# A denominator moved ahead of the turn of the carries in slots 12 and 13 of an RWKV kernel

## The chip, the cores and the metric

The kernel runs on one core of a Trainium2 chip. The metric is the device time of one execution in microseconds (us). Before the change it is 290.88 us, the median of three runs (291.6, 290.88, 290.25). The profile is that of one execution whose span is 289.9 us; all times inside the profile are counted from the start of that span.

The engines are named as in the profile: PE is the matmul engine and PEld its weight loads, DVE is VectorE, ACT is ScalarE, POOL is GpSimd and SP is SyncE. L553 stands for line 553 of the kernel.

## The reference

The inputs are `k` and `v` of shape (16, 2048, 256) and per-channel vectors `w` and `u`. For each batch and channel a recurrence runs over the 2048 steps, with a numerator `aa`, a denominator `bb` and a running maximum `pp` in the exponent:

```python
for t in range(seq_len):
    ww = u + kk
    qq = np.maximum(pp, ww)
    e1 = np.exp(pp - qq); e2 = np.exp(ww - qq)
    output[b, t, :] = (e1 * aa + e2 * vv) / (e1 * bb + e2 + 1e-08)
    ww = pp - w + kk
    qq = np.maximum(ww, kk)
    e1 = np.exp(ww - qq); e2 = np.exp(kk - qq)
    aa = e1 * aa + e2 * vv
    bb = e1 * bb + e2
    pp = qq
```

## The kernel before

The sequence is cut into a head of 32 steps and 16 stretches ("steps" of the kernel, numbered c) of 126 time steps. A stretch is worked on in four tiles of four batches each. With the two tiles of the head there are 66 tiles, numbered n: 0 and 1 are the first two of stretch 0, 2 and 3 the head, 4 and 5 the rest of stretch 0, 6 to 9 stretch 1, 10 to 13 stretch 2, and so on. The main loop runs through *slots*; slot n starts the work on tile n and finishes that on tiles some nine slots older.

What is done for one tile:

- `round_k` (DVE, L315) rounds k; `logs` (PE, L331, tile X) forms the exponents by two matmuls for each half; `exps` (ACT, L347) takes their exponentials into the tile `ez`; `times_v` (DVE, L354) multiplies by v.
- `sums` (PE, L385) adds the tile up for the carries of its stretch.
- `den` (PE, L553) forms the denominators; `log_den` (ACT, L565) and `invert` (ACT, L570) turn them into reciprocals; `num` (PE, L578 for each half) forms the numerators; `mult` (DVE, L588) multiplies, and `store` writes out.

The carries of a stretch are worked out from its sums by small operations on DVE and ACT (L422 to L495), ending in `carries` (DVE, tile `ab`, L495). They are then turned by a matmul, copied out as a `row`, and sent by small transfers into two spare rows (126 and 127) of the `ez` tiles of that stretch, so that `den` and `num` of those tiles, which read all 128 rows, take the carries in:

```python
def turn_carries(c):
    d = bank("num", [128, D]) if wide else bank("den", [128, 2, D])[:, 0]
    K(PE.matmul(d[:, 0:128], st.pop((c, "ab")).rearrange("p m q x -> p (m q x)"), It, start=True, stop=True))
    st[c, "d"] = d

def inject(c):
    row = small.tile([128, 128], BF16, tag="row", name="row")
    K(DVE.tensor_copy(row, st.pop((c, "d"))[:, 0:128]))
    for j in range(c == 0, 2):
        for h in range(2):
            p = 64 * h + 32 * j
            K(SP.dma_start(out=EZ[group_of(c, j)][TC + h:TC + h + 1, 0:2, :, :].rearrange(
                               "o q i (x c) -> o (q i x) c", c=128),
                           in_=row[p:p + 32, :]))
```

Here `EZ[group]` holds two tiles. For stretch 1 the first two transfers (j = 0) go to tiles 6 and 7, the other two to tiles 8 and 9.

Three things write to the same buffer `den` in on-chip accumulation memory: `den` itself, the turn of the carries, and a turn of the sums (L403). The pool has one buffer of it (`psd`, bufs=1) until the loads are over:

```python
def den(n):
    rl, ri = (NH, NH) if is_head(n) else (TC if is_direct(n) else 128, TC)
    d = bank("den", [128, 2, D])
    for m, r, q in (((Lh if is_head(n) else Lf), rl, 0), (Id, ri, 2)):
        for i in range(tiles_of(n)):
            K(PE.matmul(d[:, i, :], m[0:r, :], ez_of(n)[0:r, q, i, :], start=q == 0, stop=q == 2, ...))
    # ... (tiles 0 and 1 alone add their carries here, by further small matmuls)
    DEN[n] = d
```

`K` pins the order of the instructions of each engine to the order in which the program writes them. The slot loop writes them so (cut):

```python
LAG = 9
out_at = {n + (LAG - 3 if is_head(n) else LAG + 1 if n < 2 else LAG): n for n in range(NP)}
for n in range(NP + LAG + 1):
    q, qi, qp = out_at.get(n), out_at.get(n - 1), out_at.get(n - 2)
    ...
    small_work(n, "a3")
    if live:
        exps(n)
    small_work(n, "d0")
    if more and n > EARLY:
        round_k(n + 1)
    small_work(n, "p0")
    if out_qp:
        num(qp, 0)
    small_work(n, "d1"); small_work(n, "a0"); small_work(n, "p1")
    if out_qi and qi < NP - 1:
        invert(qi)
    small_work(n, "a2")
    if out_q:
        if q not in DEN:
            den(q)
        log_den(q)          # ... (cut: the last slots)
    if out_qp:
        mult(qp, 0)
    small_work(n, "d2"); ...; small_work(n, "d3"); small_work(n, "a4")
    if more:
        logs(n + 1)
    if live and out_qp:
        num(qp, 1)
    small_work(n, "p3")
    if live:
        times_v(n)
        sums(n)
    small_work(n, "p2"); small_work(n, "d4")
    if out_qp:
        mult(qp, 1)
        store(qp)
    small_work(n, "d5"); small_work(n, "p4"); small_work(n, "a1")
```

The small operations of the carries are put in by plans, as (slots after the stretch's last tile, place in the slot, function). For most stretches the plan ends so:

```python
"steady": (..., (3, "d4", carry_weights), (3, "d5", carries), (3, "p4", turn_carries), (4, "d0", inject),
           (4, "d2", state_add, 1), (4, "d4", state_decay, 1)),
```

The last tile of stretch 1 is tile 9. So its carries are made and turned at the end of slot 12, and the row is copied at the start of slot 13. By `out_at`, the denominators come in these slots: tile 0 in slot 10, tile 1 in slot 11, none in slot 12, tile 4 in slot 13, tile 5 in slot 14, tile 6 in slot 15, and from there one in each slot.

Of the kernel before, what the change touches and what calls it, by code (L numbers as in the profile page):

```python
# [22 lines left out]
def kernel(  # L23
# [593 lines left out]
    def at(slot, where, f, *args):  # L617
        later.setdefault((slot, where), []).append((f, args))
# [27 lines left out]
    for c in range(-1, NST):  # L646
        for slot, where, f, *args in PLANS["head" if c < 0 else "first" if c == 0 else
                                           "last" if c + 1 == NST else "steady"]:

            if f is copy_sums and 0 < c < NST - 1:  # L650
                where, args = "d1", (DVE,)
            at(last_of[c] + slot, where, f, c, *args)
    at(0, "d1", matrices_for_head)
    at(4, "d4", matrices_for_outputs)
    at(5, "d4", matrices_for_outputs_of_head)
    at(6, "d4", more_matrices_for_outputs)
# [121 lines left out]
```

## Time and profile before

| What | Value |
|---|---|
| Time, median of three runs | 290.88 us (290.25 to 291.6) |
| Span of the profile | 289.9 us |
| Start of the exponentials of tiles 12, 13, 14, 15, 16 on ACT | 45.74, 48.98, 53.29, 56.91, 60.99 us |
| Turn of the carries of stretch 1 on PE | 50.57 us |
| Copy of the row on DVE | 50.84 us |
| den(4), den(5), den(6): first matmul | 51.29, 54.19, 58.44 us |
| HBM traffic over the span | 352 GB/s |

A line of the timeline gives the start, the duration, the engine, the line of the kernel, the operation, the tiles (written <- read), the shapes and the count. A bracket at the end gives the time for which the engine had been idle before it and what ended that idle time. Busy time is not the same as being the bound: an engine with idle time between its instructions may still set the end by a wait, and one that is busy may lie beside the path.

### The profile page before, as it was taken

Reading aid. Unit: us, or ns where it says so; the run is one execution under the profiler, and the core shown is the slowest. Engines: PE = TensorE matmul, PEld = TensorE weight load, DVE = VectorE, ACT = ScalarE, POOL = GpSimd, SP = SyncE. Lnnn points to the kernel's source line nnn. Section 1 sums busy time; section 2 is a strip of 40 time slices with the busy share of each in tenths; the row PEclk is TensorE's granted clock in tenths of the full one; section 3 lists DMA queues with packets and bytes.
Section 4 is the critical chain, followed back from the end, with each engine's and each line's share of the span. In section 5 each row is a group of like instructions: output and inputs, shape, how many; then the busy total and the mean of one; then the engine's idle time right before and its main releaser. Section 6 shows DMA issues by size and latency. Waiting matters only on the chain.

```text
span 289.9 us, 4117 instructions
## 1 busy us (share of the span) xinstructions
PE 253.2 (87%) x1194; PEld 119.2 (41%) x1210; DVE 254.4 (88%) x529; ACT 265.5 (92%) x298; POOL 161.1 (56%) x227
## 2 busy tenths in 40 slices
PE   8888988998989998989989898989898998988950
PEld 3334444544434444434444444444343444433420
DVE  6598899899999999999999999999999999978760
ACT  7957989799999999999999999999999999998970
POOL 8695546746656666556566655666565652122530
PEclk9999999999999999999999999999999999999995
DMA  6999999999999999999999999999999999345875
GB/s 180 243 271 296 304 308 302 261 305 332 323 330 307 342 335 329 332 337 342 345 336 326 330 332 342 339 337 328 336 329 332 326 308 279 132 149 197 279 244 152
DMA packets 58971, 85.95 MB, mean 296 GB/s; under 512 B 6746, under 2 KB 43090, under 8 KB 58948
## 3 DMA queue, kind: packets, MB, share of 16 engines
q0 software_dynamic: 52672, 81.99, 102.0%
q1 hardware_dynamic: 5978, 3.41, 4.6%
q10 hardware_dynamic: 298, 0.27, 0.3%
q8 instruction: 10, 0.16, 0.2%
q14 instruction: 13, 0.11, 0.1%
HBM read 68.12 MB, written 34.05 MB: 352 GB/s over the span
## 4 chain that ended last, share of the span: by engine, by line
DVE 41%; DMA 24%; PE 15%; issue 9%; ACT 4%; POOL 3%; DVEq 0%; POOLq 0%; ACTq 0%
DMA vr<-in_v_dram 21%; DVE ez L354 17%; DVE rd L588 11%; DVE km L315 5%; PE num L578 5%; PE X L331 3%; DMA out_dram<-rd 3%; PE den L553 3%; ACT rd L565 2%; PE tot L385 2%; PE den L403 2%; DVE S L427 1%; DVE spread L540 1%; DVE ab L495 1%; DVE da L465 1%
## 5 line engine op out<-in xcount | busy, mean ns | idle before, releaser
L347 ACT ACTIVATE ez<-X 128x2048 bf16<-128x2048 f32 x58 | 108.7, 1874 | 0.4 <-PE X L331 0.4
L588 DVE TENSOR_TENSOR rd<-num,rd 128x512 f32<-128x512 f32 (+2 forms) x131 | 88.7, 684 | 4.4 <-ACT rd L570 3.6
L143 POOL DMA_DIRECT2D vr<-in_v_dram x64 | 48.9, 764 | 73.1 <-DVE ez L354 36.7
L354 DVE TENSOR_TENSOR ez<-ez,vr 126x2048 bf16<-126x2048 bf16 (+1 forms) x66 | 79.7, 1209 | 2.6 <-DMA vr<-in_v_dram 2.6
L608 POOL DMA_DIRECT2D out_dram<-rd x63 | 56.2, 892 | 39.5 <-issue 11.0
L565 ACT ACTIVATE rd<-den 128x1024 f32<-128x1024 f32 (+3 forms) x67 | 66.9, 998 | 4.6 <-PE den L553 2.6
L570 ACT ACTIVATE rd<-rd 128x1024 f32<-128x1024 f32 (+3 forms) x67 | 69.4, 1035 | 0.3
L578 PE MATMUL num<-ez,LfN 128*128 128x512 bf16 (+1 forms) x128 | 49.2, 384 | 7.6 <-DVE rd L588 7.6
L331 PE MATMUL X<-km,NLE 128*128 128x512 f32 x128 | 50.6, 477 | 2.2 <-DVE km L315 1.0
L578 PE MATMUL num<-ez,IdN 126*128 126x512 bf16 (+1 forms) x131 | 49.8, 380 | 0.0
L121 POOL DMA_DIRECT2D kr<-in_k_dram x60 | 45.7, 761 | 6.1 <-issue 2.4
L315 DVE CAST km<-kr 126x1024 fp32r<-126x1024 f32 x64 | 47.5, 742 | 0.9 <-DMA kr<-in_k_dram 0.8
L331 PE MATMUL X<-km,NLZ 128*128 128x512 f32 x128 | 40.4, 396 | 0.2 <-ACT ez L345 0.2
L553 PE MATMUL den<-ez,Id 126*128 126x512 bf16 (+1 forms) x131 | 39.1, 378 | 0.8
L553 PE MATMUL den<-ez,Lf 128*128 128x512 bf16 (+1 forms) x112 | 34.6, 378 | 0.1
L385 PE MATMUL tot<-ez,OHV 126*32 126x512 bf16 x128 | 25.2, 384 | 5.2 <-DVE ez L354 5.1
L331 PEld LDWEIGHTS X<-km,NLE 128*128 128x128 f32 x128 | 23.2, 189 | 13.7 <-ACT lf L422 1.3
L331 PEld LDWEIGHTS X<-km,NLZ 128*128 128x128 f32 x128 | 24.0, 188 | 6.2 <-ACT ez L345 0.6
L385 PE MATMUL tot<-ez,OHE 128*32 128x512 bf16 x128 | 25.2, 390 | 0.0
L578 PEld LDWEIGHTS <-LfN 128*128 128x128 bf16 (+1 forms) x128 | 12.3, 96 | 22.9 <-issue 20.5
L553 PEld LDWEIGHTS <-Lf 128*128 128x128 bf16 (+1 forms) x128 | 12.4, 98 | 18.7 <-issue 7.1
L553 PEld LDWEIGHTS <-Id 126*128 126x128 bf16 (+1 forms) x131 | 12.7, 97 | 15.7
(113 smaller groups left out, 213.2 us busy)
## 6 DMA issues: line engine op xcount, KB each, us to landing
out_dram<-rd POOLq DMA_DIRECT2D x60, 512.0 KB, 7.4
kr<-in_k_dram POOLq DMA_DIRECT2D x56, 512.0 KB, 8.0
vr<-in_v_dram POOLq DMA_DIRECT2D x60, 256.0 KB, 7.3
kr<-in_k_dram SPq DMA_DIRECT2D x4, 512.0 KB, 5.0
kr<-in_k_dram POOLq DMA_DIRECT2D x4, 504.0 KB, 9.3
out_dram<-rd POOLq DMA_DIRECT2D x3, 504.0 KB, 6.8
vr<-in_v_dram POOLq DMA_DIRECT2D x4, 252.0 KB, 8.0
ez<-row SPq DMA_DIRECT2D x62, 8.0 KB, 5.2
```

Source lines behind the costliest of these rows:

```text
L143: K(POOL.dma_start(out=vr_of[n][0:r, :, :], in_=v[4 * p:4 * p + 4, t0:t0 + r, :].rearrange("n t d -> t n d")))
L315: K(DVE.tensor_copy(KM[n][0:r, 0:i, :], kr_of.pop(n)[0:r, 0:i, :]))
L331: K(PE.matmul(X[q][:, i, :], m[0:kr, :], km[0:kr, i, :], start=True, stop=True))
L347: K(SC.activation(ez_of(n)[:, 0:4:2], X[2][:, :, 0:i, :], ACT.Exp))
L354: K(DVE.tensor_mul(ez[0:r, 1:4:2], ez[0:r, 0:4:2], vb[0:r].unsqueeze(1).broadcast_to([r, 2, i, D])))
L385: K(PE.matmul(TOT[c][y:y + 32], m[0:r, :], ez_of(n)[0:r, q, i, :], start=n == first_of[c], stop=n == last_of[c] or (head and i == 1), tile ...
L553: K(PE.matmul(d[:, i, :], m[0:r, :], ez_of(n)[0:r, q, i, :], start=q == 0, stop=q == 2, skip_group_check=True))
L565: K(SC.activation(RD[n][0:r, a:b, :], DEN[n][0:r, a:b, :], ACT.Ln, scale=RS))
L570: K(SC.activation(RD[n][0:r, a:b, :], RD[n][0:r, a:b, :], ACT.Exp, scale=-1.0))
L578: K(PE.matmul(d, m[0:r, :], ez_of(n)[0:r, q, i, :], start=q == 1, stop=q == 3, skip_group_check=True))
L588: K(DVE.tensor_mul(RD[n][0:r, i, :], NUM.pop((n, i))[0:r, :], RD[n][0:r, i, :]))
L608: K(eng.dma_start(out=out[4 * p + a:4 * p + b, t0:t0 + r, :].rearrange("n t d -> t n d"), in_=o[0:r, a:b, :]))
```

## The change

In stretch 1 alone, the turn of the carries moves from the end of slot 12 to slot 13, behind num(1,1), and the copy of the row moves with it, behind `times_v(13)`. The denominator of tile 4 moves from the middle of slot 13 to the end of slot 12, ahead of the turn. As both use the one den buffer, the turn now follows the log of that denominator, where before the denominator followed the copy of the row. It is for the wait in which ACT stands before the log of den(4). No instruction is added or removed.

```diff
         for slot, where, f, *args in PLANS["head" if c < 0 else "first" if c == 0 else
                                            "last" if c + 1 == NST else "steady"]:
 
+            if c == 1 and f in (turn_carries, inject):
+                slot, where = 4, "p3" if f is turn_carries else "d4"
+
             if f is copy_sums and 0 < c < NST - 1:
                 where, args = "d1", (DVE,)
             at(last_of[c] + slot, where, f, c, *args)
     at(0, "d1", matrices_for_head)
+    at(12, "p2", den, 4)
     at(4, "d4", matrices_for_outputs)
```

The order of the instructions on PE changes so, from the sums of tile 12 to those of tile 13:

```
before: sums(12), turn, num(1,0), den(4), logs(14), num(1,1), sums(13)
after:  sums(12), den(4), num(1,0), logs(14), num(1,1), turn, sums(13)
```

and on DVE, from the carries to the rounding of tile 15:

```
before: carries, copy of the row, round_k(14), mult(1,0), state_add, times_v(13), state_decay, mult(1,1), round_k(15)
after:  carries, round_k(14), mult(1,0), state_add, times_v(13), copy of the row, state_decay, mult(1,1), round_k(15)
```

ACT has the same order in both.

## The prediction

> **What bounds the kernel now.** I read the busy line first, then the busy time by stretch, then the order of time around slot 13, engine by engine, and last the four small transfers that carry the turned carries.
>
> ```profile
> PE 253.2 (87%) x1194; PEld 119.2 (41%) x1210; DVE 254.4 (88%) x529; ACT 265.5 (92%) x298; POOL 161.1 (56%) x227
> ```
>
> The busy time by stretch (us, then busy us of PE, PEld, DVE, ACT, POOL, clock, DMA share, GB/s):
>
> ```profile
> 40.00:45.74 5.74, 5.23 (x32) 2.54 (x31) 5.23 (x13) 4.66 (x7) 3.71 (x5) 1.00 1.24 306
> 45.74:53.29 7.55, 6.16 (x39) 3.46 (x38) 7.12 (x15) 6.00 (x8) 4.97 (x8) 1.00 1.07 259
> 53.29:60.99 7.70, 7.37 (x40) 3.35 (x39) 6.35 (x13) 7.70 (x10) 3.95 (x6) 1.00 1.14 286
> 76.80:92.60 15.80, 14.48 (x70) 6.93 (x69) 14.96 (x30) 15.69 (x20) 9.62 (x12) 1.00 1.16 318
> 92.60:108.40 15.80, 14.48 (x70) 6.94 (x69) 14.86 (x30) 15.50 (x18) 9.74 (x12) 1.00 1.17 336
> ```
>
> The reader is to see that ACT (ScalarE) is the bound from 53 us on: 7.70 of 7.70 us, then 15.50 to 15.69 of 15.80 us for each four slots, at the same pace to 250 us. So time lost or won on ACT near slot 13 should stay to the end. The one large hole of that region lies in 45.74 to 53.29, where ACT is busy 6.00 of 7.55 us. ACT in order of time:
>
> ```profile
> 48.98 1.86 ACT L347 ACTIVATE ez<-X 128x2048 bf16<-128x2048 f32 x1
> 52.36 1.03 ACT L565 ACTIVATE rd<-den 128x1024 f32<-128x1024 f32 x1 [1.52 <-PE den L553]
> 53.29 1.88 ACT L347 ACTIVATE ez<-X 128x2048 bf16<-128x2048 f32 x1
> ```
>
> These are the exponentials of tile 13, the log of denominator 4, and the exponentials of tile 14. The hole is 1.52 us, ended by den(4). What den(4) waits for is seen on DVE and PE:
>
> ```profile
> 48.36 1.22 DVE L354 TENSOR_TENSOR ez<-ez,vr 126x2048 bf16<-126x2048 bf16 x1
> 50.23 0.28 DVE L495 TENSOR_TENSOR ab<-AB,phi 128x128 bf16<-128x128 f32 x1
> 50.84 0.29 DVE L508 CAST row<-den 128x128 bf16<-128x128 f32 x1 [0.33 <-PE den L503]
> 51.64 0.68 DVE L588 TENSOR_TENSOR rd<-num,rd 128x512 f32<-128x512 f32 x1
> 52.37 1.22 DVE L354 TENSOR_TENSOR ez<-ez,vr 126x2048 bf16<-126x2048 bf16 x1
> 53.96 0.69 DVE L588 TENSOR_TENSOR rd<-num,rd 128x512 f32<-128x512 f32 x1 [0.24 <-PE num L545]
> ```
>
> ```profile
> 49.63 0.39 PE L385 MATMUL tot<-ez,OHV 126*32 126x512 bf16 x2
> 50.57 0.23 PE L503 MATMUL den<-It,ab 128*128 128x128 bf16 x1 [0.54 <-DVE ab L495]
> 51.72 0.60 PE L553 MATMUL den<-ez,Id 126*128 126x512 bf16 x2
> 52.62 0.63 PE L331 MATMUL X<-km,NLZ 128*128 128x512 f32 x2
> ```
>
> The turn of the carries (L503) uses the only den buffer, and it idles PE for 0.54 us until the carries (L495) are made. DVE copies the turned row out (L508, ends 51.13), and only then may den(4) write: it ends at 52.32 and X(14) at 53.25.
>
> **The other end of the row.** The row goes by four 8 KB transfers from SyncE into ez, the first two for tiles 6 and 7. Their first reader is den(6) in slot 15:
>
> ```profile
> 58.44 0.59 PE L553 MATMUL den<-ez,Lf 128*128 128x512 bf16 x2
> ```
>
> The queries for the row's transfers, over the whole run:
>
> ```profile
> L512 SPq DMA_DIRECT2D ez<-row x62: 502/590/1206, 34.4 to 268.5; - x62
> DMA to landing us min/median/max: 1.9/5.2/6.9
> ```
>
> Asked one by one, the four of this step are issued at 51.19, 51.74, 52.44 and 53.45 and take 4.4, 4.7, 6.9 and 6.8 us. So the pair that den(6) needs is there at 51.74 + 4.7 = 56.4, and den(6) starts at 58.44: **slack 2.0 us**. This is the number on which I decide.
>
> [...] behind the waiting turn, num(1,0) stands still although its bank came free at 50.31. So a den(6) that waits holds X(16) behind it. [...] the same 8 KB take 4.4 to 6.9 us here and as little as 1.9 us at the end, when loads are over.
>
> **The change part by part.** No instruction is added or removed. Three things move.
>
> 1. den(4) (4 matmuls) goes from slot 13 to the end of slot 12, ahead of the turn, where its buffer has been free since the log of den(1) ended at 45.52. The sums of tile 12 begin their last pair at 49.63; elsewhere the next matmul starts 0.32 us after that pair (57.04 to 57.37), so den(4) starts at 49.95. Matmuls of this width start 0.22 us apart (58.44, 58.65, 58.87, 59.09), so the last starts at 50.61 and ends at 50.99. The log can start at 51.03, not 52.36: ACT waits about 0.2 us, not 1.52.
>
> 2. PE then runs num(1,0) (two of 0.22 us and four short ones of 0.055) from 50.83; X(14) starts at about 51.5 and ends after 1.2 us (55.40 to 56.56 elsewhere), at 52.7. exp(14) starts at 52.75, not 53.29: **0.54 us won on ACT**. It is less than the hole, as X(14) becomes the limit; it is the 0.54 us for which PE stood idle.
>
> 3. DVE loses its wait of 0.33 us and the copy of 0.29, but then waits for num(1,0), which ends at 51.65, not 51.45. The product at 51.64 starts at 51.69, and the product with v (52.37) at 52.42. The copy of the row now comes after that one, at 53.55 to 53.85; the turn itself, behind num(1,1) on PE, is ready at about 53.4, and the log that it must follow ended at 52.1, so the wait in the title costs nothing. The product at 53.96 starts at 53.88: DVE wins 0.08 us. X(15) waits for k rounded on DVE, so at exp(15) only 0.1 to 0.3 of the 0.54 us is left.
>
> 4. **The price.** The row is ready at 53.85, not 51.13: 2.7 us later, against a slack of 2.0. Transfers start at 53.91 and 54.46. With 4.7 us the second lands at 59.2; with 5.8, the median of the four, at 60.3; with 6.9, like those issued in this very stretch (52.44, 53.45), at 61.4. den(6), ready at about 58.36, then starts at 59.2, 60.3 or 61.4.
>
> 5. From den(6) to ACT: it needs 1.03 us (58.44 to 59.47), the log follows 0.04 us later, and exp(16) starts 1.22 us after the log (59.77 to 60.99, with two small exponentials between). So exp(16) starts 2.29 us after den(6): at 61.5, 62.6 or 63.7, against 60.99 now. That is **0.5, 1.6 or 2.7 us lost**. The 0.54 us won lies before this wait and is swallowed by it. The second pair, for tiles 8 and 9, would land at 62 to 63 and is read in slot 17 (66.99): no wait.
>
> After slot 16 ACT is full, so what is lost there stays; perhaps 0.1 to 0.2 us comes back, as ACT has idle bits of 0.2 us at 68.05 and 74.69. I take the middle, 1.6, less 0.2, and lean toward the short landing, since the first pairs of later steps take 4.7 to 5.2 us where the trace has their landing (82.9 to 210 us): about +1.2 us. 290.88 + 1.2 = 292.1.
>
> **Rivals.** *The hole is simply filled.* exp(14) wins 0.54 us and all behind it moves up: 290.4, or 290.7 if DVE's 0.1 to 0.3 us is what survives. For it: ACT is the bound, with 7.70 of 7.70 us. Against it: the row must land within 3.9 us of its second issue, and under load none of the first pairs did (4.4 us is the shortest I looked at near this step). *Given back without a loss.* The landing takes about 4.4 us and den(6) stands only some 0.5 us; exp(16) is then within 0.2 us of now: 290.9. *A longer wait.* The transfers meet the bulk loads and take 6.9 us: 293.4. *The turn waits for the log of den(4).* It would idle PE, but the log ends 1.1 us before PE comes to the turn: no effect.
>
> **Range and chances.** From a short landing (+0.3) to a long one (+2.5) with repeats that themselves spread from 290.25 to 291.6: 290.8 to 293.4. Two per cent are 5.8 us, which none of the cases reaches: within 2% at 0.98, faster and slower 0.01 each. Within these 2%, I give four in five to a small loss.
>
> **What would show it.** The wait of 1.52 us before the log at 52.36 shrinks to about 0.2 us; exp(14) starts near 52.75; the copy of the row starts near 53.5; PE has a new idle of 0.8 to 2.9 us before den(6), ended by the row's transfer; exp(16) starts at 61.5 to 63.7; from there the pace is again 15.8 us for four slots. I am wrong if den(6) starts before 58.9, which needs the row copied before 53 us or a landing in about 4 us, or if the delay at slot 16 melts away by 100 us.

## The result and the profile after

The changed kernel takes 295.98 us (median of six runs, 294.07 to 296.61), against 290.86 us before (six runs, 290.25 to 291.6): a ratio of 1.0166 with a 95% interval of 1.0134 to 1.0199. It is slower by 5.1 us: a loss within two per cent, as foretold, but larger than the prediction allowed (292.1, at most 293.4). The ratios, here and below, are worked out from single runs, without those over 1.5% above the fastest of their kernel, and so are not quotients of the medians.

The busy line of the changed kernel's page, and its busy time by stretch (columns as before). The first two stretches run from exp(12) to exp(14) and to exp(15), the third from there to exp(16); the fourth lies in the steady part:

```profile
PE 254.6 (86%) x1194; PEld 119.9 (41%) x1210; DVE 254.5 (86%) x529; ACT 266.2 (90%) x298; POOL 160.3 (54%) x227
```

```profile
45.10:52.04 6.94, 6.10 (x38) 3.37 (x37) 6.26 (x14) 6.10 (x8) 4.08 (x7) 1.00 1.14 274
52.04:55.89 3.85, 3.58 (x21) 1.64 (x20) 3.85 (x7) 3.73 (x3) 3.11 (x5) 1.00 1.11 268
55.89:64.85 8.96, 5.30 (x19) 2.63 (x17) 3.88 (x8) 4.36 (x6) 2.36 (x4) 0.73 1.14 315
96.00:112.00 16.00, 14.67 (x70) 7.04 (x70) 15.03 (x31) 15.69 (x18) 9.82 (x13) 1.00 1.17 338
```

Nearly all the harm lies in the third line. From exp(15) to exp(16) took 4.08 us before (56.91 to 60.99) and takes 8.96 us now, with every engine but PE idle for more than half of it, and with a mean PE clock of 0.73. ACT of the changed kernel in order of time:

```profile
50.40 1.02 ACT L565 ACTIVATE rd<-den 128x1024 f32<-128x1024 f32 x1 [0.20 <-PE den L553]
52.04 1.88 ACT L347 ACTIVATE ez<-X 128x2048 bf16<-128x2048 f32 x1 [0.62 <-PE X L331]
...
63.14 1.02 ACT L565 ACTIVATE rd<-den 128x1024 f32<-128x1024 f32 x1 [4.23 <-PE den L553]
...
64.85 1.88 ACT L347 ACTIVATE ez<-X 128x2048 bf16<-128x2048 f32 x1 [0.37 <-PE X L331]
```

The hole of 1.52 us before the log of den(4) is gone (0.20 us, then 0.62 us for X(14)). In its place ACT waits 4.23 us before the log of den(6). DVE and PE show the way there:

```profile
51.05 0.69 DVE L588 TENSOR_TENSOR rd<-num,rd 128x512 f32<-128x512 f32 x1 [0.57 <-PE num L545]
51.79 1.22 DVE L354 TENSOR_TENSOR ez<-ez,vr 126x2048 bf16<-126x2048 bf16 x1
52.93 0.28 DVE L508 CAST row<-den 128x128 bf16<-128x128 f32 x1
53.26 0.69 DVE L588 TENSOR_TENSOR rd<-num,rd 128x512 f32<-128x512 f32 x1
```

```profile
57.35 0.38 PE L578 MATMUL num<-ez,IdN 126*128 126x512 bf16 x1
61.24 1.01 PE L553 MATMUL den<-ez,Lf 128*128 128x512 bf16 x2 [3.50 <-DMA ez<-row]
62.04 1.06 PE L553 MATMUL den<-ez,Id 126*128 126x512 bf16 x2
62.54 1.41 PE L331 MATMUL X<-km,NLE 128*128 128x512 f32 x2
```

The row is copied at 52.93. PE is through with num(4,0) at 57.73 and stands 3.50 us until the row has landed. Then each pair of den matmuls takes 1.01 to 1.06 us, where it took 0.59 and 0.60 before. The clock of PE (second column from the left is the length; the last three are clock, DMA share and GB/s) fell to half inside the wait, at 60.06 us:

```profile
59.00:60.00 1.00, 0.00 (x0) 0.00 (x0) 0.93 (x5) 0.00 (x0) 0.00 (x0) 1.00 1.29 281
60.00:61.00 1.00, 0.00 (x0) 0.00 (x0) 0.87 (x1) 0.00 (x0) 0.00 (x0) 0.53 1.09 392
63.00:64.00 1.00, 1.00 (x4) 0.81 (x3) 0.00 (x0) 0.86 (x1) 0.00 (x0) 0.50 1.33 306
```

That last row must be read with care: PE is "busy" for the whole microsecond, but at a clock of 0.50 the two X matmuls begun at 62.54 take 1.41 us, where the like pair at 103.45, at a clock of 1.00, takes 0.80. The transfers of the row, asked for the first pair alone:

```profile
L512 SPq DMA_DIRECT2D ez<-row x2: 503/1024/1545, 53.3 to 53.8; - x2
...
DMA to landing us min/median/max: 5.7/6.5/7.3
```

The second one is issued at 53.82 and takes 7.3 us: it lands at 61.10. In the kernel before it took 4.7 us. The bulk load issued just ahead of it (v of tile 19, issued at 53.31) lands at 61.06, within 0.04 us of it.

### The profile page after: what moved, and what is told of

It reads as the page before. It is cut to its first block, busy times and chain, and to the rows that moved or that the text cites. A ratio compares the mean times of both kernels' runs of the same rounds, so it can differ in the third digit from the quotient of the medians.

```text
span 294.9 us, 4116 instructions
## 1 busy us (share of the span) xinstructions
PE 254.6 (86%) x1194; PEld 119.9 (41%) x1210; DVE 254.5 (86%) x529; ACT 266.2 (90%) x298; POOL 160.3 (54%) x227
## 4 chain that ended last, share of the span: by engine, by line
DVE 39%; DMA 25%; PE 15%; issue 10%; ACT 7%; POOL 1%; DVEq 0%; SPq 0%; POOLq 0%; ACTq 0%
DMA vr<-in_v_dram 17%; DVE ez L354 15%; DVE rd L588 10%; DVE km L315 5%; PE num L578 5%; DMA out_dram<-rd 3%; ACT rd L565 3%; PE den L553 3%; PE X L331 3%; DMA ez<-row 2%; DMA kr<-in_k_dram 2%; ACT ez L347 2%; PE tot L385 2%; DVE ab L495 1%; PE den L403 1%
## 5 line engine op out<-in xcount | busy, mean ns | idle before, releaser
L608 POOL DMA_DIRECT2D out_dram<-rd x63 | 55.6, 882 | 46.4 <-issue 12.1
L565 ACT ACTIVATE rd<-den 128x1024 f32<-128x1024 f32 (+3 forms) x67 | 66.9, 998 | 9.1 <-PE den L553 5.3
L331 PE MATMUL X<-km,NLE 128*128 128x512 f32 x128 | 51.2, 482 | 2.7 <-ACT ez L345 0.8
```

Source lines behind the costliest of these rows:

```text
L331: K(PE.matmul(X[q][:, i, :], m[0:kr, :], km[0:kr, i, :], start=True, stop=True))
L565: K(SC.activation(RD[n][0:r, a:b, :], DEN[n][0:r, a:b, :], ACT.Ln, scale=RS))
L608: K(eng.dma_start(out=out[4 * p + a:4 * p + b, t0:t0 + r, :].rearrange("n t d -> t n d"), in_=o[0:r, a:b, :]))
```

## The experiments

Theory A is that of the prediction: the row now reaches tiles 6 and 7 too late for den(6), and what follows from that wait is the whole loss. Theory B is that the new order on PE and DVE itself costs. The kernel before was run beside each group and takes 291.35 to 291.36 us there (25 to 39 runs); ratios are against it.

**Late send.** The order of the kernel before stays; only the transfers go out late, from a holding tile.

```diff
 def inject(c):
+    if c == 1:  # copied out of the den buffer at the old time
+        st["held"] = tiny.tile([128, 128], BF16, tag="held", name="held")
+        K(DVE.tensor_copy(st["held"], st.pop((c, "d"))[:, 0:128]))
+    else:
+        send(c)
+
+def send(c):
     row = small.tile([128, 128], BF16, tag="row", name="row")
-    K(DVE.tensor_copy(row, st.pop((c, "d"))[:, 0:128]))
+    K(DVE.tensor_copy(row, st.pop("held") if c == 1 else st.pop((c, "d"))[:, 0:128]))
     # ... the transfers
+at(13, "d4", send, 1)
```

> The kernel before, with its order of den(4) and turn untouched; the turned row of stretch 1 is copied out of the den buffer at the old time, into a holding tile, and a second small copy at the place where the changed kernel copies (behind the product with v of slot 13) feeds the four transfers. Only the time of sending is late, by about 2.5 us; added is one copy of 128x128 on DVE, about 0.1 to 0.2 us. Theory A (the late landing before den(6), with the PE clock that drops behind the wait, is the cost): PE idle 2.5 to 4 us before den(6), and 294.5 to 296.5 us. Theory B (the new order on PE and DVE, with den(4) ahead and the turn behind num(1,1), is the cost): no more than 0.2 us over the kernel before, 290.9 to 291.2.

Measured: 295.58 us, ratio 1.0127 (1.0083 to 1.0170). The added copy takes 0.19 us. PE of this run before den(6):

```profile
61.78 0.68 PE L560 MATMUL den<-ez,Lf 128*128 128x512 bf16 x2 [3.69 <-DMA ez<-row]
62.25 1.06 PE L560 MATMUL den<-ez,Id 126*128 126x512 bf16 x2
```

The old order with a late row has the whole loss, the wait and the slow pair behind it. Theory B falls.

**No read.** The changed kernel, but den and num of tiles 6 and 7 read 126 rows. It leaves the carries of stretch 1 out of these two tiles, so that nothing waits for the row there.

```diff
-rl, ri = (NH, NH) if is_head(n) else (TC if is_direct(n) else 128, TC)
+rl, ri = (NH, NH) if is_head(n) else (TC if is_direct(n) or n in (6, 7) else 128, TC)
```

> The changed kernel, where den and num of tiles 6 and 7 read 126 rows in place of 128 and so leave the carries of stretch 1 out of these two tiles; their first reader then waits for no transfer. Theory A: the idle time before den(6) is gone, exp(14) stays about 0.6 us early, and the time is 290.3 to 290.8, 0 to 0.5 us under the kernel before. Theory B (the new order): still 294 to 296.

Measured: 290.95 us, ratio 0.9982 (0.9966 to 0.9997). PE at the same place:

```profile
57.39 0.38 PE L578 MATMUL num<-ez,IdN 126*128 126x512 bf16 x1
57.76 0.59 PE L553 MATMUL den<-ez,Lf 126*128 126x512 bf16 x2
```

No wait, and no loss, though the row was no quicker (it took 7.3 us and landed at 61.18). So the wait of den(6) and what hangs on it is all the harm. As control, the same edit in the kernel before:

> A control: the kernel before, where den and num of tiles 6 and 7 read 126 rows and so leave the carries of stretch 1 out of these tiles. The kernel before had no wait for the transfers, so this should change nothing: within 0.2 us of it. Then the 0.4 us that the changed kernel without this wait was under the kernel before are what the filled hole is worth; if the control is 0.4 us under it too, the filled hole is worth nothing.

Measured: 291.16 us, ratio 0.9985 (0.9953 to 1.0017). The control is as far under the kernel before as the changed kernel without its wait. So these runs show no gain in time from the filled hole.

**Turn only.** One part alone: without `at(12, "p2", den, 4)`, so that den(4) stays in slot 13.

> One part of the change alone: the turn and the copy of the row go to slot 13 as in the changed kernel, den(4) stays at its old place behind num(1,0). Theory A: the row is as late as in the changed kernel, so the time is the same within 0.5 us, 295.3 to 296.5; the log of den(4) starts some 0.7 us later than in the changed kernel but exp(14), bound by X(14), at the same time. If it is the early den(4) that costs: back at 291.

Measured: 295.54 us, ratio 1.0126 (1.0089 to 1.0163). The early den(4) is harmless; the late turn has the loss. One part of the expectation failed: exp(14) starts 7.28 us after exp(12), against 6.94 with the early den(4) and 7.55 before. So more than half of the time won at exp(14), 0.34 of 0.62 us, comes from the early den(4), and not all from the late turn.

**Clock held.** The changed kernel with matmuls of zeros in the wait: `at(15, "a2", idle, psd, 12)`.

> The changed kernel with 12 matmuls of zeros (2.6 us at 0.22 us each) put on PE right ahead of den(6), where it stands idle for 3.5 us. If the drop of the PE clock to half behind that wait is a cost of its own: den(6) again takes about 1.0 us in place of 1.9, exp(16) follows 2.3 us after den(6) in place of 3.6, and the time is 1.0 to 1.4 us under the changed kernel, 294.6 to 295.0. If the clock does not matter to the path (ACT would be late anyway): within 0.3 us of the changed kernel.

Measured: 294.95 us, ratio 1.0103 (1.0072 to 1.0134). In its profile the row came still later than in the changed kernel (8.5 us, at 62.31), and yet:

```profile
57.73 2.75 PE L219 MATMUL idle<-zeros 128*128 128x512 bf16 x12
62.45 0.38 PE L553 MATMUL den<-ez,Lf 128*128 128x512 bf16 x1 [1.97 <-DMA ez<-row]
62.88 0.59 PE L553 MATMUL den<-ez,Id 126*128 126x512 bf16 x2
```

The pair takes 0.59 us again, and exp(16) follows den(6) by 2.30 us in place of 3.61. (One record of the first pair is missing here.) So 1.3 us of the changed kernel's profile are the clock. To see it in time, both stand once more in one group:

> The changed kernel once more, as it is, beside the three others of this group. Theory A says: PE stands 2.5 to 4 us before den(6) again, ended by the second transfer at about 61 us. Open is the loss of 1.1 us between 220 and 250 us in the first profile, where ACT waits for buffers of results not yet stored: if it belongs to the change it comes again, if it is chance it does not. 294.5 to 296.5 us.

> The 12 matmuls of zeros ahead of den(6) once more, now beside the changed kernel itself: if the broken PE clock costs, 0.8 to 1.4 us under the changed kernel of this group, and 2.3 us from den(6) to exp(16) in the profile; if not, within 0.3 us.

Measured: the changed kernel 294.60 us (six runs, 292.72 to 296.29), ratio 1.0116 (1.0071 to 1.0161); with zeros 293.87 us (ten runs), ratio 1.0089 (1.0058 to 1.0119). The difference of 0.7 us has the expected sign, but the intervals overlap: in time the cost of the clock is not settled. One reason is seen in the profile of the changed kernel of this group, which is its shortest run:

```profile
60.45 0.59 PE L553 MATMUL den<-ez,Lf 128*128 128x512 bf16 x2 [1.96 <-DMA ez<-row]
60.88 0.60 PE L553 MATMUL den<-ez,Id 126*128 126x512 bf16 x2
```

Here the row took 5.7 us, PE stood 1.96 us and kept its clock. So the two profiles of the changed kernel differ in how long the transfer takes and in whether the clock breaks. The mean PE clock of whole runs suggests how often it breaks: it is 0.988 in this run and 0.974 to 0.984 in the changed kernel's eleven others, as in the profiles with a broken clock (0.978 to 0.983); in all sixteen runs with zeros it is 0.987 to 0.992.

**Why is the landing so late?** Three runs move the sending or what is issued beside it. The first is the late send with the second copy ahead of the product with v (`at(13, "d2", send, 1)`):

> The kernel before with the holding tile, where the second copy and the transfers come ahead of the product with v of slot 13, some 1.2 us later than in the kernel before and 1.2 us sooner than in the late send. If a transfer took 4.7 us as in the kernel before, the second would land near 57.6, before den(6) at 58.44: 290.9 to 291.3. If the transfers sent from 52.4 us on land at 59.3 to 60.3 whatever they are (as the third and fourth did in the kernel before, 6.9 us), den(6) stands 1 to 2 us: 292 to 293.5. So the slack was less than 2.0 us if it is the second.

Measured: 294.17 us, ratio 1.0076 (1.0042 to 1.0109). That is above what I expected. The row was sent 0.8 us sooner than in the late send, took 6.5 us and landed at 60.65; PE stood 1.74 us, and its clock broke (0.60 in the mean from 61 to 62 us, 0.50 in the two behind), which my expectation left out. After exp(12), this row lands 2.0 us sooner than that of the late send, but no sooner than that of the changed kernel's second profile (14.56 against 14.46 us), which is sent 0.7 us later. One profile of each can't tell what the sooner sending is worth.

The second is the changed kernel with the turn right behind `logs(14)` and the copy ahead of `times_v(13)`:

```diff
-slot, where = 4, "p3" if f is turn_carries else "d4"
+slot, where = 4, "p5" if f is turn_carries else "d6"   # p5: behind logs(n + 1); d6: ahead of times_v(n)
```

> The changed kernel with the turn right behind the matmuls of X(14) and the copy of the row ahead of the product with v of slot 13: the row is sent about 0.9 us sooner, DVE does its copy before the product. Theory A: the second transfer lands 0.5 to 1 us sooner than in the changed kernel (near 60.3), PE stands about 2.5 us, and the time is 293.5 to 295.

Measured: 292.48 us (the seven runs of the ratio, 290.69 to 294.43; two more took 295.12 and 295.51), ratio 1.0036 (0.9999 to 1.0073), somewhat better than I expected. The profile is that of the longest run, which the ratio leaves out; its row landed at 60.85. That the row came in time in the short runs is likely, but no profile shows it.

The third holds back the bulk loads:

```diff
+if n == 15:
+    load(19)
+    load(20)
-if n + AHEAD < NP:
+if n + AHEAD < NP and n not in (13, 14):
     load(n + AHEAD)
```

> The changed kernel, where the loads of tiles 19 and 20 are issued behind the store of tile 1 (with those of tile 21) in place of slots 13 and 14: about 0.75 MB less is queued ahead of the row's transfers. If their 5.7 to 8.5 us are the bulk loads queued with them: the second lands within 5 us of its issue, PE stands less than 1.1 us before den(6) with its clock unbroken, and the time is 290.3 to 292. If the length comes from elsewhere (the two rows, the SyncE issue): 6 us and more as before, and 295 to 296.5.

Measured: 291.68 us, ratio 1.0014 (0.9995 to 1.0033). POOL of the changed kernel, from the loads of tile 19 to the next store, and then of this run:

```profile
52.26 0.77 POOL L121 DMA_DIRECT2D kr<-in_k_dram  x1
53.31 0.75 POOL L143 DMA_DIRECT2D vr<-in_v_dram  x1 [0.27 <-DVE row L508]
54.52 0.76 POOL L608 DMA_DIRECT2D out_dram<-rd  x1 [0.47 <-issue]
```

```profile
51.95 0.76 POOL L608 DMA_DIRECT2D out_dram<-rd  x1
54.95 0.75 POOL L608 DMA_DIRECT2D out_dram<-rd  x1 [2.23 <-ACT ez L347]
```

Its first pair of transfers, and den(6):

```profile
L512 SPq DMA_DIRECT2D ez<-row x2: 502/870/1237, 53.7 to 54.3; - x2
...
DMA to landing us min/median/max: 4.4/4.6/4.7
```

```profile
58.76 0.59 PE L553 MATMUL den<-ez,Lf 128*128 128x512 bf16 x2 [0.60 <-DVE km L315]
```

Nothing was changed about the row. With no load issued between 51.95 and 54.95 it lands at 58.63, in place of 61.10. The profile names DVE for the wait of 0.60 us, but den(6) starts 0.13 us after the landing. The last bulk transfer now issued ahead of it, the store at 51.95, landed at 58.26. So with the loads of tile 19 issued just ahead of it the transfer took 7.3 us, and without them 4.4 us. Both together:

> Both of the former, the sooner turn and the held loads. If both act on the landing and add up: it lands by 57.5, no wait before den(6), and the time is 290.2 to 291.0, at or a little under the kernel before; the most that the filled hole on ACT gave without any wait was 0.4 us (290.95 against 291.36).

Measured: 291.42 us, ratio 1.0001 (0.9985 to 1.0017). The row lands at 57.67 and den(6) does not wait. The whole loss is gone, and nothing is won, where I had expected 290.2 to 291.0. The control, held loads in the kernel before:

> A control for the held loads: the kernel before with the loads of tiles 19 and 20 held back in the same way. Its row had 2.0 us to spare and the loads are needed only four to five slots later: within 0.3 us of the kernel before. If it is faster by 0.3 us or more, the held loads themselves help, and the sum of sooner turn and held loads hides a loss of the change.

Measured: 290.99 us (the 21 runs of the ratio), ratio 0.9982 (0.9961 to 1.0003): no difference that these runs can show. Here the second transfer took 6.8 us in spite of the held loads. It is sent at 51.18, before the loads of tile 19 would be issued; those of tile 18, issued 1.5 and 0.7 us ahead of it, stayed. No version beat the kernel before clearly.

The profiles side by side, in us after the start of exp(12), which takes out how the first slots of each run went (the kernel before: exp(12) at 45.74):

| Kernel | second transfer sent | landed | PE idle before den(6) | den(6) to exp(16) | exp(16) |
|---|---|---|---|---|---|
| before | 6.00 | 10.72 | 0 | 2.55 | 15.25 |
| before, no read | 6.00 | 12.94 | (not awaited) | 2.54 | 15.26 |
| before, held loads | 6.00 | 12.76 | 0.20 | 2.35 | 15.25 |
| changed | 8.72 | 16.00 | 3.50 | 3.61 | 19.75 |
| changed, again | 8.72 | 14.46 | 1.96 | 2.30 | 16.89 |
| changed, turn only | 8.91 | 15.38 | 2.70 | 3.30 | 18.81 |
| before, late send | 8.79 | 16.55 | 3.69 | 3.27 | 19.96 |
| before, mid send | 8.03 | 14.56 | 1.74 | 3.23 | 17.93 |
| changed, clock held | 8.72 | 17.21 | 1.97, behind 12 zeros | 2.30 | 19.65 |
| changed, clock held, again | 8.71 | 15.87 | 0.64, behind 12 zeros | 2.30 | 18.31 |
| changed, held loads | 8.71 | 13.09 | 0.60 | 2.30 | 15.52 |
| changed, sooner and held | 7.91 | 12.63 | 0 | 2.31 | 15.26 |
| changed, no read | 8.72 | 16.04 | (not awaited) | 2.38 | 15.01 |

den(6) is needed 12.6 to 12.7 us after exp(12). Where the clock breaks, den(6) to exp(16) is 3.2 to 3.6 us, elsewhere 2.3 to 2.55.

## Why the prediction was wrong

**The way was right.** The order of events came as foretold, and the steps on the engines to within 0.1 us. From exp(12), the log of den(4) was predicted at 5.29 us and came at 5.30; the copy of the row at 7.81, and came at 7.83; the product behind it 0.08 us sooner than before, and came 0.06 us sooner. I gave 0.54 us to exp(14), and 0.62 came. What is lost at slot 16 stays, as foretold: the exponentials of the changed kernel's profile run 4.15 to 4.17 us behind those of the kernel before from 73 to 223 us.

**The step that failed is the fourth, "The price": the landing.** I laid three cases side by side, 4.7, 5.8 and 6.9 us, took the middle one and then leaned "toward the short landing", because later steps took 4.7 to 5.2 us. In the six profiles that send at the changed kernel's time with the loads as they are (changed, clock held twice, no read, late send, and changed again) the transfer took 7.3, 8.5, 7.2, 7.3, 7.8 and 5.7 us: five of the six are above the longest case. In turn only, sent 0.2 us later, it took 6.5 us. The transfers sent nearest to that moment in the trace of the kernel before (52.44 and 53.45, 6.9 and 6.8 us) were the better model, not the pairs of later steps. With the loads of this stretch held back, the transfer took 4.4 us; why those of later steps were quicker is not shown. (By that step's own landings PE would stand 0.8 to 3.0 us before den(6), not 0.8 to 2.9.)

The middle case did come, in the second profile of the changed kernel: the row landed 14.46 us after exp(12), where the middle case has 14.6, exp(16) came at 16.89, where it has 16.9, and that run took 292.72 us. The eleven other runs of the changed kernel took 293.94 us or more. So the case that I took as the middle was near the lucky end.

**The slack was not a number but a draw.** I decided on 2.0 us, from one profile. With the same order and the same moment of sending, the no-read control landed at 12.94 us where 12.7 are needed, and the control with held loads at 12.76, so that den(6) stood 0.20 us. So the old moment of sending leaves at times no slack at all, though no profile of the kernel before itself shows that. (Two of its 39 runs in the last group took 294.2 and 294.41 us, with a mean PE clock of 0.983 and 0.984 like the changed kernel's; why is not shown.)

**The fifth step, den(6) to ACT, was mis-sized where the wait is long.** I took 2.29 us, which came where PE kept its clock (2.30). In the first profile it was 3.61 us: behind 3.50 us of standing still, PE ran at half its clock until 66.9 us. The length of standing still alone does not decide in these runs: 1.96 us kept the clock, 1.74 us broke it, and so did 2.70, 3.50 and 3.69. The slow stretch is 6.83 us long in the first profile (60.06 to 66.89), and about 3.4 us in turn only and in mid send, worked out from the mean clock of each microsecond. What sets the moment at which the clock breaks is not shown. I had the wait in view and forgot its second effect.

So the first profile's exp(16), 19.75 us after exp(12) where the middle case has 16.86, is 2.89 us too late for two reasons: den(6) starts 1.6 us later than in that case, as the landing took 7.3 us and not 5.8, and the way from den(6) to exp(16) is 1.3 us longer, by the broken clock.

**The sum of the first profile**, exp(12) to exp(16): den(6) starts 3.44 us later than before (16.14 against 12.70), and from there to exp(16) is 1.06 us longer (3.61 against 2.55): 4.50 us, which is 19.75 less 15.25. Of the rest of the 5.0 us between the two spans, 0.64 us is taken off by a quicker start before slot 12, and some 1.1 us comes after exp(16), mostly from 227 us on, where ACT waits 1.7 us in all for buffers of results not yet stored. This did not come again in the second profile of the changed kernel. It stood in the profiles with a broken clock (0.2 to 1.7 us), but also in one whose clock was whole and which has no loss, the no-read control (0.8 us). So it is not shown to belong to the change; why it comes is open.

**The rivals.** "The hole is simply filled" fell in both ways: den(6) waits, and without that wait the gain melts. In the no-read run exp(14) is 0.62 us early, exp(15) 0.38, exp(16) 0.24 and exp(20) 0.07 (31.21 us after exp(12) against 31.28), probably because DVE and PE are nearly as full as ACT (86%, 86% and 90% of the first profile's span); no run tests that. The 0.1 to 0.3 us that I left at exp(15) was near, but I had not followed it to the end. "Given back without a loss" needed a landing in about 4.4 us; that came with the held loads alone, and there den(6) stood 0.60 us and the time was not clearly longer (1.0014). "A longer wait" (6.9 us, 293.4) was the one that held, and was still too short. The turn behind the log cost nothing, as foretold.

## What to carry to other kernels

- When a change makes a producer later, look at the far end of what it feeds before the near end: a gap of 1.5 us was filled, and a transfer that seemed to have 2.0 us to spare became a wait of 2.0 to 3.5 us.
- The time of a small transfer beside bulk loads was no constant here: 5.7 to 8.5 us in six profiles. Take it from transfers issued near the same moment, from several profiles, and take the long ones for the slack.
- The new wait on PE was charged twice in the profiles where the clock broke behind it (den(6) to exp(16) took 3.2 to 3.6 us, and 2.3 where it held), and its length alone did not tell whether it would: 1.74 us broke the clock, 1.96 us did not. And a gap on the fullest engine need not be worth its length: here 1.3 us of it were filled, and no time was won, with two other engines nearly as full (86% each in the changed kernel, against 90%).

## What the runs showed of the hardware

The same 8 KB transfer, sent at the same point of the program (8.7 us after exp(12)), took 5.7 to 8.5 us in six profiles, with loads of 512 KB (k) and 256 KB (v) issued just ahead of it, and 4.4 us in one profile where these were held back by about 3 us. It landed 0.04 us after the last load issued ahead of it in the first profile of the changed kernel, and 1.15 us before it in the second. The PE clock fell to half behind 1.74 us of standing still in one run and stayed whole behind 1.96 us in another; in three profiles where it fell (turn only, mid send, and the first of the changed kernel) it was back at full 2.8, 3.8 and 5.6 us after work had begun again.
